# The adaLN partition sums of the dense layer, from float32 vectors or from two float32r limbs

## The chip, the cores and the metric

The kernel runs on one core of one Trainium2 chip. The metric is the device time of one execution in microseconds (us). The engines are TensorE (PE, with PEld for its weight loads), VectorE (DVE), ScalarE (ACT), GpSimd (POOL) and SyncE (SP), whose queue issues nearly all transfers.

## The reference, cut to what matters

A diffusion backbone of two layers works on 256 latent tokens and 256 context tokens of width 1024. Each layer has an adaLN-modulated RMSNorm, a mixer of two branches, a second adaLN-modulated norm and a feed-forward: a dense SwiGLU of width 2816 in layer 0, eight experts in layer 1. The change touches only how the adaLN modulation is summed:

```python
def adaln(cvec, w_mod, b_mod, n_chunks):
    m = jax.nn.silu(cvec) @ w_mod[:, :n_chunks * D_MODEL] + b_mod[:n_chunks * D_MODEL]
    return jnp.split(m, n_chunks, axis=-1)
```

`w_mod` is 2 x 1024 x 6144. There are two conditioning vectors, that of the latent and that of the context tokens; the context needs fewer chunks in layer 1.

## The kernel before

The products of the layers are made in three float32r matmuls each: weights and activations are cut into a high and a low limb (`wh`, `wl` and `hh`, `hl`), and high x high, high x low and low x high are added in PSUM (L212 to L214). A limb pair costs a ScalarE copy to float32r (`wh` L169) and a VectorE subtraction (`wl` L181). A class `Stream` hands out weight halves of 128 columns; the low limb of half i+2 and the high limb of half i+3 are issued behind the matmuls of half i, which are called a group below: 24 matmuls of 512 columns in the gate and up products and in the first two parts of the down product, 18 in the third.

The dense layer runs in three parts of 8, 8 and 6 blocks of 128 hidden columns. In each part, for two blocks at a time, two gate groups end in `sg` (ScalarE, L1189) and two up groups in `af` (VectorE, L1194), `ah` (ScalarE, L1195) and `al` (VectorE, L1196). Then come the down products of the part, which end in additions to `xT` (L1084). Three PSUM banks turn in these products.

Beside this runs the adaLN of later stages, as a background queue (`bgq["mod"]`). Its generator `adaln_units` goes through units of 512 columns of `w_mod`: eight loads of 128 x 512 (`rawm`, L303, 256 KB each, eight buffers), each multiplied by a scalar per partition and accumulated into `acc` on VectorE, once per vector (L318 the first time, then L320). A finished `acc` still has to be summed over the 128 partitions. That is what `finish` does: a matmul (L268) whose stationary operand is a slice of `one_col`, zero but for one column of ones, so that vector m of a list lands in row m of `psr`. When the list is complete, ScalarE copies the rows (`rw`, L273), TensorE transposes them (L278) and VectorE adds the bias into `mod` (L283).

In the dense layer there are three lists (L1165): units (0,10) and (0,11) with two vectors each, (1,0) to (1,3) with two, (1,4) to (1,11) with one; 20 vectors. `finish` for a unit is reached one step after the second load of the next unit, and for the last unit of a list two steps after its last accumulation.

The order of all engines' instructions is written out by the program (a manual schedule). After every three product matmuls `tick` adds `pace["mod"]` to a credit, and at each full unit of credit the generator runs to its next `yield`: one step. At 0.5 that is one step in two ticks. `need(0, 11)` behind the first part's gate and up products and `drain("mod")` behind the down products run what is left at once. The lists take 169 steps, and the layer has 494 ticks ahead of the drain.

Of the kernel before, what the change touches and what calls it, by code (L numbers as in the profile page):

```python
# [11 lines left out]
F32 = mybir.dt.float32  # L12
F32R = mybir.dt.float32r
I32 = mybir.dt.int32
AF = mybir.ActivationFunctionType
OP = mybir.AluOpType
# [54 lines left out]
def ap_of(t, off, pat):  # L71
    return bass.AP(tensor=t.tensor, offset=t.offset + off, ap=pat)
# [3 lines left out]
def hybrid_kernel(ctx, tc, x, c, ctx_in, c_ctx, w_mod, b_mod, norm1_g, norm2_g, w_in, sink, w_fourier,  # L76
# [3 lines left out]
    V, A, P_, G, S = nc.vector, nc.scalar, nc.tensor, nc.gpsimd, nc.sync  # L80
# [6 lines left out]
    const = ctx.enter_context(tc.tile_pool(name="const", bufs=1))  # L87
# [9 lines left out]
    pace = {"attn": 1.0, "mod": 0.5}  # L97
# [130 lines left out]
    one_col = const.tile([128, 15], F32, name="one_col")  # L228
    G.memset(one_col, 0.0)
    G.memset(one_col[:, 7:8], 1.0)  # L230
    mhalf = const.tile([128, 4], F32, name="mhalf")
    G.memset(mhalf, -0.5)

# [3 lines left out]
    mod = [const.tile([128, 48, 2], F32, name=f"mod{l}") for l in range(2)]  # L237
# [12 lines left out]
    g2col = lambda l: cols[:, 112 + l * 8:112 + (l + 1) * 8]  # L250


    def adaln_units(ps_pool, todo, raw_at, nraw, acc_at, nacc, queue, rows=None, may=None):


        total, first, nv0 = sum(t[2] for t in todo), todo[0], todo[0][2]
        gathered = [0, None]

        def finish(l, u, nv, acc):
            if rows:  # L260
                while may and not may():
                    yield
                if gathered[1] is None:
                    gathered[1] = ps_pool.tile([8, 512], F32, name="psr", tag="s", bufs=2)
                ps = gathered[1]
                for v in range(nv):
                    m = gathered[0]
                    P_.matmul(ps[:total, :], one_col[:, 7 - m:7 - m + total], acc[v], start=(m == 0),  # L268
                              stop=(m == total - 1))
                    gathered[0] += 1  # L270
                if gathered[0] == total:
                    rw = rows()
                    A.activation(rw[:total, :], ps[:total, :], AF.Copy)  # L273
                    yield
                    nu = len(todo)
                    pt = ps_pool.tile([128, 4, nu, nv], F32, name="psm", tag="t", bufs=NT_)
                    for ct in range(4):
                        P_.transpose(pt[:, ct].rearrange("p u v -> p (u v)"),  # L278
                                     rw[:total, ct * 128:(ct + 1) * 128], ident[:total, :total])
                    u0 = first[1]  # L280
                    for v in range(nv):
                        as_uc = lambda t: t.rearrange("p (u c) -> p u c", c=4)
                        V.tensor_tensor(as_uc(mod[l][:, 4 * u0:4 * (u0 + nu), v]),  # L283
                                        pt[:, :, :, v].rearrange("p c u -> p u c"),
                                        as_uc(bcol(l)[:, 4 * u0:4 * (u0 + nu)]), op=OP.add)
                    for t in todo:
                        done[t[0], t[1]] = True
                return
            ps = ps_pool.tile([128, 4, 2], F32, name="psm", tag="t", bufs=NT_)
            for ct in range(4):  # L290
                for v in range(nv):
                    P_.matmul(ps[:, ct, v:v + 1], acc[v][:, ct * 128:(ct + 1) * 128], ones[:, 0:1],
                              start=True, stop=True)
            V.tensor_tensor(mod[l][:, 4 * u:4 * u + 4, :nv], ps[:, :, :nv],
                            bcol(l)[:, 4 * u:4 * u + 4, None].to_broadcast([128, 4, nv]), op=OP.add)
            done[l, u] = True
            return
            yield

        def load(i):  # L300
            l, u, nv = todo[i // 8]
            r = raw_at(i)
            queue.dma_start(r, ap_of(w_mod, l * D * NMOD * D + (i % 8) * NMOD * D + u * 512,  # L303
                                 [[KC * NMOD * D, 128], [1, 512]]))
            return r

        late = []
        raws = [load(i) for i in range(nraw)]
        yield
        for i in range(8 * len(todo)):  # L310
            (l, u, nv), kc = todo[i // 8], i % 8
            if kc == 0:
                acc = acc_at(i // 8)
            r = raws.pop(0)
            for v in range(nv):
                s = cvec[:, kc, v:v + 1]
                if kc == 0:
                    V.tensor_scalar(acc[v], r, s, None, op0=OP.mult)  # L318
                else:
                    V.scalar_tensor_tensor(acc[v], r, s, acc[v], op0=OP.mult, op1=OP.add)  # L320
                yield
            if i + nraw < 8 * len(todo):
                raws.append(load(i + nraw))
            if kc == 7:
                if nacc == 1:
                    yield
                    yield from finish(l, u, nv, acc)
                    yield
                    yield
                else:  # L330
                    late.append((l, u, nv, acc))
            if late and kc == 1:
                yield from finish(*late.pop(0))
        yield
        while late:
            yield from finish(*late.pop(0))
# [341 lines left out]
    with ExitStack() as st:  # L678
        ld = st.enter_context(tc.tile_pool(name="ld", bufs=1))
        rows = ld.tile([128, 128], F32, name="rows")  # L680
# [448 lines left out]
    with ExitStack() as st:  # L1129
# [3 lines left out]

        mx_ = [modp.tile([128, 512], F32, name=f"mx{i}") for i in range(4)]
        bgq["mod"].append(adaln_units(psA, [(0, u, 2) for u in (4, 5)], lambda i: mx_[2 + i % 2], 2,
                                      lambda i: mx_[:2], 1, G))

        def more_mod():
            ring = r16.tile([128, 8, T2], F32, name="ring", tag="ro")
            bgq["mod"].append(adaln_units(psA, [(0, u, 2) for u in range(6, 10)], lambda i: ring[:, i % 8, :], 8,  # L1140
                                          lambda i: (mx_[:2], mx_[2:])[i % 2], 2, S,
                                          lambda: rw_of[0].tile([8, 512], F32, name="rw", tag="rw"),
                                          lambda: rw_of))
# [17 lines left out]
        load_tab()  # L1161
        dump("x1", xT)
        modp2 = st.enter_context(tc.tile_pool(name="modp2", bufs=1, side="right"))
        pace["mod"] = 0.5
        for todo in ([(0, u, 2) for u in range(10, 12)], [(1, u, 2) for u in range(4)],  # L1165
                     [(1, u, 1) for u in range(4, 12)]):
            bgq["mod"].append(adaln_units(
                psA, todo, lambda i: modp2.tile([128, 512], F32, name="rawm", tag="rawm", bufs=8), 8,
                lambda i: [modp2.tile([128, 512], F32, name="acc", tag="acc", bufs=4) for _ in range(2)], 2, S,
                lambda: modp2.tile([8, 512], F32, name="rw", tag="rw")))  # L1170
        ff = st.enter_context(tc.tile_pool(name="ff", bufs=1))
        ssum = ff.tile([128, 512], F32, name="ssum", tag="ssum")
        sq = lambda n: ff.tile([128, n], F32, name="sq", tag="sq", bufs=2)
        for a, b in PARTS:
            ah = r16.tile([128, 8, T2], F32R, name="ah", tag="ro")
            al = r16.tile([128, 8, T2], F32R, name="al", tag="ro")
            for j in range(a, b, 2):
                sg = []
                for br in range(2):
                    for k in range(2):  # L1180
                        if j == 0 and br == 0:
                            ps = first[k]
                        else:
                            wh, wl = stream.take()
                            ps = psA.tile([128, 512], F32, name="psp", tag="mm", bufs=3)
# [5 lines left out]
                        else:  # L1191
                            i = j - a + k
# [120 lines left out]
    class Flow:  # L1313
# [24 lines left out]
        def high(self):  # L1338

            if not self.todo:  # L1340
                i = self.n_high
                if i == len(self.us):
                    return
                self.hi[i] = hlp.tile([128, 2048], F32R, name="eh", tag="wh", bufs=3)
                src = self.raw[i].parts(4 if i == len(self.us) - 1 else 2 if i < 2 else 1)
                wd = 2048 // len(src)
                self.todo = [(i, x, slice(wd * k, wd * k + wd), k == len(src) - 1) for k, x in enumerate(src)]
            i, x, sl, last = self.todo.pop(0)
            with self.if_split(i):
                A.activation(self.like(self.hi[i][:, sl], x), x, AF.Copy)  # L1350
            self.owed.append((i, x, sl, last))
            if last:
                self.n_high += 1
# [664 lines left out]
```

## Time and profile before

| | |
|---|---|
| median of 3 runs | 1889.34 us (1888.78 to 1890.16) |
| the profiled execution | 1892.03 us, span 1890.1 us |
| mean granted TensorE clock | 0.987 |
| busy: PE, DVE, ACT, POOL | 1808.0, 1505.8, 1131.6, 64.7 us |
| dense layer | from 369 to 735 us of the span |
| its background sums (first to last) | 401.7 to 623.7 us |

Times in the trace are microseconds from the span's start. In a timeline row the first number is the start and the second the duration (of a run of equal instructions, of all of them); matmuls overlap, so their cost is read from the distances of starts, and not from durations. What stands in brackets is the engine's idle time before the instruction and what ended it.

### The profile page before, as it was taken

Reading aid. Unit: us, or ns where it says so; the run is one execution under the profiler, and the core shown is the slowest. Engines: PE = TensorE matmul, PEld = TensorE weight load, DVE = VectorE, ACT = ScalarE, POOL = GpSimd, SP = SyncE. Lnnn points to the kernel's source line nnn. Section 1 sums busy time; section 2 is a strip of 40 time slices with the busy share of each in tenths; the row PEclk is TensorE's granted clock in tenths of the full one; section 3 lists DMA queues with packets and bytes.
Section 4 is the critical chain, followed back from the end, with each engine's and each line's share of the span. In section 5 each row is a group of like instructions: output and inputs, shape, how many; then the busy total and the mean of one; then the engine's idle time right before and its main releaser. Section 6 shows DMA issues by size and latency. Waiting matters only on the chain. (4 is left out here: it accounts for less than half of the span.)

```text
span 1890.1 us, 27281 instructions
## 1 busy us (share of the span) xinstructions
PE 1808.0 (96%) x9701; PEld 1503.6 (80%) x9701; DVE 1505.8 (80%) x1772; ACT 1131.6 (60%) x1280; POOL 64.7 (3%) x95
## 2 busy tenths in 40 slices
PE   7999999999999999999998999999999999999996
PEld 5788877877777888899877778778887788888874
DVE  6788896578777335787788998999889988889897
ACT  5664522422122223665487878888778887787785
POOL 3200000200000001100000000000000000000000
PEclk9999999999999999999899999999999999999998
DMA  9323463265577223434889999999999999999993
GB/s 297 104 58 98 134 202 100 95 213 187 178 241 249 90 79 100 135 112 141 305 331 343 387 364 375 408 403 408 353 344 406 399 399 336 337 356 376 368 403 125
DMA packets 223312, 488.57 MB, mean 258 GB/s; under 512 B 11426, under 2 KB 107938, under 8 KB 223140
## 3 DMA queue, kind: packets, MB, share of 16 engines
q1 hardware_dynamic: 221860, 482.11, 70.5%
q0 software_dynamic: 1280, 4.20, 0.8%
q8 instruction: 105, 1.72, 0.4%
q14 instruction: 67, 0.55, 0.1%
HBM read 485.22 MB, written 1.05 MB: 257 GB/s over the span
## 5 line engine op out<-in xcount | busy, mean ns | idle before, releaser
L1374 DVE TENSOR_TENSOR el<-raw,eh 128x2048 fp32r<-128x2048 f32 (+2 forms) x332 | 723.8, 2210 | 85.7 <-ACT eh L1350 76.9
L1350 ACT ACTIVATE eh<-raw 128x2048 fp32r<-128x2048 f32 (+2 forms) x332 | 607.6, 1858 | 95.2 <-PE pgt L1831 63.8
L212 PE MATMUL psp<-hh,wh 128*128 128x512 f32 (+1 forms) x704 | 260.8, 370 | 2.6 <-ACT U L954 1.8
L214 PE MATMUL psp<-hh,wl 128*128 128x512 f32 (+1 forms) x704 | 256.1, 364 | 4.9 <-DVE wl L181 4.8
L213 PE MATMUL psp<-hl,wh 128*128 128x512 f32 (+1 forms) x704 | 255.3, 363 | 0.0
L181 DVE TENSOR_TENSOR wl<-raw,wh 128x1024 fp32r<-128x1024 f32 (+1 forms) x152 | 182.3, 1206 | 41.8 <-PE psp L214 20.8
L169 ACT ACTIVATE wh<-raw 128x1024 fp32r<-128x1024 f32 (+1 forms) x152 | 156.4, 1039 | 61.2 <-DMA raw<-in_w_down_d 24.7
L212 PEld LDWEIGHTS psp<-hh,wh 128*128 128x128 f32 x704 | 134.3, 191 | 30.9 <-issue 9.9
L214 PEld LDWEIGHTS psp<-hh,wl 128*128 128x128 f32 x704 | 134.1, 190 | 27.9 <-DVE wl L181 7.4
L213 PEld LDWEIGHTS psp<-hl,wh 128*128 128x128 f32 x704 | 134.2, 191 | 19.2 <-issue 0.5
L1831 PE MATMUL py<-el,eah 128*128 128x256 f32 (+1 forms) x712 | 125.7, 314 | 8.3 <-DVE el L1374 7.3
L1831 PEld LDWEIGHTS py<-el,eah 128*128 128x128 f32 x712 | 101.7, 189 | 36.4 <-DVE el L1374 28.1
L1831 PE MATMUL py<-eh,eah 128*128 128x512 f32 x440 | 120.6, 396 | 0.0
L320 DVE SCALAR_TENSOR_TENSOR acc<-rawm,cvec,acc 128x512 f32<-128x512 f32 x140 | 99.8, 747 | 1.4
L1831 PE MATMUL pup<-el,xh 128*128 128x256 f32 (+1 forms) x560 | 94.4, 307 | 4.6 <-DVE el L1374 4.5
L1831 PEld LDWEIGHTS pup<-el,xh 128*128 128x128 f32 x560 | 80.7, 188 | 19.6 <-DVE el L1374 11.1
L1831 PE MATMUL pgt<-el,xh 128*128 128x256 f32 (+1 forms) x480 | 84.9, 315 | 11.3 <-DVE el L1374 10.7
L1831 PE MATMUL pup<-eh,xh 128*128 128x512 f32 x336 | 94.0, 401 | 0.0
L1831 PEld LDWEIGHTS pgt<-el,xh 128*128 128x128 f32 x480 | 70.1, 191 | 27.6 <-DVE el L1374 19.6
L1831 PEld LDWEIGHTS py<-eh,eah 128*128 128x128 f32 x440 | 78.7, 188 | 14.4 <-ACT eh L1350 0.8
L1831 PE MATMUL pgt<-eh,xh 128*128 128x512 f32 x296 | 83.4, 404 | 0.7 <-ACT xh L1462 0.7
L1195 ACT ACTIVATE ah<-af 128x512 fp32r<-128x512 f32 x22 | 13.9, 632 | 99.8 <-DVE af L1194 99.8
(379 smaller groups left out, 3236.1 us busy)
## 6 DMA issues: line engine op xcount, KB each, us to landing
raw<-in_w_gate_e SPq DMA_DIRECT2D x111, 1024.0 KB, 7.5
raw<-in_w_down_e SPq DMA_DIRECT2D x110, 1024.0 KB, 8.0
raw<-in_w_up_e SPq DMA_DIRECT2D x109, 1024.0 KB, 8.3
rawm<-in_w_mod SPq DMA_DIRECT2D x112, 256.0 KB, 5.3
raw<-in_w_in SPq DMA_DIRECT2D x26, 1024.0 KB, 5.4
raw<-in_w_gate_d SPq DMA_DIRECT2D x11, 1024.0 KB, 5.3
raw<-in_w_up_d SPq DMA_DIRECT2D x11, 1024.0 KB, 5.5
mraw<-in_w_mod SPq DMA_DIRECT2D x16, 512.0 KB, 8.4
```

The costliest lines, as they stand in the source:

```text
L169: A.activation(h[:, :n, :], src, AF.Copy)
L181: self.eng.tensor_tensor(lo[:, :n, :], src, h[:, :n, :].bitcast(F32), op=OP.subtract)
L212: P_.matmul(ps, wh[:, k, :], ah, start=(start and i == 0), stop=False)
L213: P_.matmul(ps, wh[:, k, :], al, start=False, stop=False)
L214: P_.matmul(ps, wl[:, k, :], ah, start=False, stop=(stop and i == n - 1))
L320: V.scalar_tensor_tensor(acc[v], r, s, acc[v], op0=OP.mult, op1=OP.add)
L1195: A.activation(ah[:, i, :], t, AF.Copy)
L1350: A.activation(self.like(self.hi[i][:, sl], x), x, AF.Copy)
L1374: V.tensor_tensor(self.like(self.lo[i][:, sl], x), x, self.like(self.hi[i][:, sl], x).bitcast(F32), op=OP.subtract)
L1831: P_.matmul(ps[:, a:b], x[:, k, :], w[:, c + a:c + b], start=(start and ps_id[i] not in seen), stop=(stop and ps_id[i] not in ps_id[i + 1: ...
```

## The change

The vectors of the dense layer are cut into two float32r limbs before they are summed: a ScalarE copy makes the high one, a VectorE subtraction the low one, out of a ring of three buffers `limb`. Two steps later two float32r matmuls per vector, with a float32r copy of `one_col` as the stationary operand, take the place of the float32 one. The pace of the background queue in the dense layer goes from 0.5 to 0.55. The sums of the mixer, which use the same function, stay as they are.

```diff
@@ -228,6 +228,8 @@
     one_col = const.tile([128, 15], F32, name="one_col")
     G.memset(one_col, 0.0)
     G.memset(one_col[:, 7:8], 1.0)
+    one_row = const.tile([128, 15], F32R, name="one_row")
+    V.tensor_copy(one_row, one_col)
@@ -250,7 +252,7 @@
-    def adaln_units(ps_pool, todo, raw_at, nraw, acc_at, nacc, queue, rows=None, may=None):
+    def adaln_units(ps_pool, todo, raw_at, nraw, acc_at, nacc, queue, rows=None, may=None, high=None):
@@ -265,8 +267,17 @@
                 for v in range(nv):
                     m = gathered[0]
-                    P_.matmul(ps[:total, :], one_col[:, 7 - m:7 - m + total], acc[v], start=(m == 0),
-                              stop=(m == total - 1))
+                    x = [(one_col, acc[v])]
+                    if high:
+                        hi, lo = high()
+                        A.activation(hi, acc[v], AF.Copy)
+                        V.tensor_tensor(lo, acc[v], hi.bitcast(F32), op=OP.subtract)
+                        x = [(one_row, hi), (one_row, lo)]
+                        yield
+                        yield
+                    for i, (one, a) in enumerate(x):
+                        P_.matmul(ps[:total, :], one[:, 7 - m:7 - m + total], a, start=(m == 0 and i == 0),
+                                  stop=(m == total - 1 and i == len(x) - 1))
                     gathered[0] += 1
@@ -1161,13 +1172,14 @@
-        pace["mod"] = 0.5
+        pace["mod"] = 0.55
...
-                lambda: modp2.tile([8, 512], F32, name="rw", tag="rw")))
+                lambda: modp2.tile([8, 512], F32, name="rw", tag="rw"),
+                high=lambda: [modp2.tile([128, 512], F32R, name="limb", tag="limb", bufs=3) for _ in range(2)]))
```

## Rows read from the trace of the kernel before

**Rows 1.** The page's first part: busy us, share of the span, instructions.
```profile
PE 1808.0 (96%) x9701; PEld 1503.6 (80%) x9701; DVE 1505.8 (80%) x1772; ACT 1131.6 (60%) x1280; POOL 64.7 (3%) x95
```

**Rows 2.** By stretch: length, busy PE, PEld, DVE, ACT, POOL; clock, DMA share, GB/s.
```profile
401.40:452.60 51.20, 51.20 (x219) 39.21 (x218) 37.28 (x53) 14.91 (x19) 0.00 (x0) 1.00 0.54 180
...
500.30:597.50 97.20, 97.20 (x405) 72.45 (x404) 69.17 (x95) 24.27 (x31) 0.00 (x0) 1.00 0.70 233
...
1100.00:1400.00 300.00, 286.35 (x1593) 240.56 (x1592) 270.56 (x172) 240.58 (x200) 0.00 (x0) 1.00 0.99 379
```

**Rows 3.** Waits from 379 to 640: who for whom, us in total, times, longest.
```profile
DVE al L1196 <- ACT ah L1195: 11.2, 16, 0.7
...
PEld psp L214 <- DVE wl L181: 2.1, 3, 1.2
...
PE psp L214 <- DVE wl L181: 0.8, 1, 0.8
```

**Rows 4.** Instructions of tile psr, 379 to 640: ns min/median/max, first and last start.
```profile
L268 PE MATMUL psr<-acc,one_col x40: 592/592/597, 401.7 to 623.7; 128*8 128x512 f32 x32, 128*4 128x512 f32 x8
L273 ACT ACTIVATE rw<-psr x3: 588/588/588, 423.3 to 624.4; 8x512 f32<-8x512 f32 x2, 4x512 f32<-4x512 f32 x1
```

**Rows 5.** Timeline of PE around the first pair and up to the second.
```profile
401.39 0.39 PE L214 MATMUL psp<-hh,wl 128*128 128x512 f32 x1
401.71 1.88 PE L268 MATMUL psr<-acc,one_col 128*4 128x512 f32 x4
...
403.86 0.40 PE L213 MATMUL psp<-hl,wh 128*128 128x512 f32 x1
...
421.11 0.39 PE L214 MATMUL psp<-hh,wl 128*128 128x512 f32 x1
```

**Rows 6.** Timeline of PE around a single vector.
```profile
539.92 0.39 PE L214 MATMUL psp<-hh,wl 128*128 128x512 f32 x1
...
541.53 0.39 PE L213 MATMUL psp<-hl,wh 128*128 128x512 f32 x1
```

**Rows 7.** Timeline of PE in the start-up: float32r matmuls with four stationary columns.
```profile
46.39 0.39 PE L811 MATMUL psq<-hl,wh 128*128 128x512 f32 x1
46.61 0.28 PE L716 MATMUL psg<-mh,c 128*4 128x256 f32 x1
...
47.90 0.28 PE L716 MATMUL psg<-ml,c 128*4 128x256 f32 x1
```

**Rows 8.** Groups by line, 379 to 640: busy us, mean ns, idle before.
```profile
L320 DVE SCALAR_TENSOR_TENSOR acc<-rawm,cvec,acc 128x512 f32<-128x512 f32 x140 | 99.8, 747 | 1.4
...
L1196 DVE TENSOR_TENSOR al<-af,ah 128x512 fp32r<-128x512 f32 x16 | 11.1, 693 | 11.2 <-ACT ah L1195 11.2
...
L1195 ACT ACTIVATE ah<-af 128x512 fp32r<-128x512 f32 x16 | 10.1, 632 | 74.1 <-DVE af L1194 74.1
```

**Rows 9.** Timeline of DVE at the start of the layer's accumulations.
```profile
379.49 0.88 DVE L318 TENSOR_SCALAR acc<-rawm,cvec 128x512 f32<-128x512 f32 x2 [8.15 <-DMA rawm<-in_w_mod]
...
392.51 1.21 DVE L181 TENSOR_TENSOR wl<-raw,wh 128x1024 fp32r<-128x1024 f32 x1
393.64 2.73 DVE L320 SCALAR_TENSOR_TENSOR acc<-rawm,cvec,acc 128x512 f32<-128x512 f32 x4
```

**Rows 10.** Timeline of PE at the same place.
```profile
382.23 0.50 PE L214 MATMUL psp<-hh,wl 128*128 128x512 f32 x1 [0.79 <-DVE wl L181]
```

**Rows 11.** Timeline of DVE, 406 to 426 us.
```profile
406.57 0.69 DVE L1194 TENSOR_TENSOR af<-sg,psp 128x512 f32<-128x512 f32 x1
407.96 0.69 DVE L1196 TENSOR_TENSOR al<-af,ah 128x512 fp32r<-128x512 f32 x1 [0.70 <-ACT ah L1195]
...
425.26 0.24 DVE L283 TENSOR_TENSOR mod<-psm,cols 128x8 f32<-128x8 f32 x2 [8.38 <-PE psm L278]
```

**Rows 12.** Timeline of DVE from the span's start: its first instruction.
```profile
5.01 0.18 DVE L700 TENSOR_TENSOR c<-cvec,c 128x16 fp32r<-128x16 f32 x1 [5.01 <-ACT c L699]
```

**Rows 13.** Waits of SP's queue, 735 to 905: the first expert loads (L1224).
```profile
SPq L1224 <- PE psp L214: 4.9, 4, 3.7
```

## The prediction

> **What bounds the kernel now.** I read the page's busy times first [rows 1], then the busy times by stretch [rows 2], then who waited for whom between 379 and 640 us [rows 3], and last the order of time around single places. The reader is to see this. TensorE is busy for 96% of the span [rows 1], but that is an average; what counts is the dense layer, where the change sits. There TensorE is busy for all of 51.20 us and all of 97.20 us at the full granted clock (1.00, the 2.4 GHz level), while VectorE is busy 71 to 73% and ScalarE 25 to 29% [rows 2]. In 261 us TensorE and its weight loads wait for VectorE's low limbs for 2.1 + 0.8 us only [rows 3]. So in this stage a TensorE microsecond removed is a microsecond of the kernel, as long as the other two engines stay ahead.
>
> **Removed: the float32 sums.** Between 401.7 and 623.7 us the profile has 40 instructions `psr<-acc,one_col` of float32 [rows 4]: 20 vectors, two instructions each. Their price is what they push apart. The ordinary rate first: from the L213 at 403.86 to the L214 at 421.11 lie 76 product matmuls, (421.11 - 403.86)/76 = 0.227 us each [rows 5]. A pair of vectors: from the L214 at 401.39 to the L213 at 403.86 are 2.47 us, in which two ordinary matmul steps lie (0.454), so the pair costs 2.016 us [rows 5]. A single vector: 539.92 to 541.53 is 1.61, less 0.454, 1.156 us [rows 6]. The units (0,10), (0,11) and (1,0) to (1,3) are pairs, (1,4) to (1,11) are single: 6 x 2.016 + 8 x 1.156 = 21.3 us. A pair has two instructions more than a single vector and costs 2.016 - 1.156 = 0.860 more, 0.430 each; 40 of them are 17.2 us. What is left of a single one, 1.156 - 0.860 = 0.296, comes once for each of 14 insertions, 4.1 us in all: the switch between float32r and float32.
>
> **Added on TensorE: 40 float32r matmuls**, 128 x 512 with a stationary of 4 or 8 columns. The trace has float32r matmuls with 4 columns and 256 moving columns: from 46.61 to 47.90 us eleven steps, 0.117 us each, and the step from a product matmul to the first of them is 0.22 us, an ordinary one [rows 7]. So few columns cost no extra and there is no switch. For 512 columns I take the 0.227 of the products: 40 x 0.227 = 9.1 us. Net on TensorE: 21.3 - 9.1 = 12.2 us less. The dear end of this price is that each insertion keeps its 0.296 us, and there are now 20 insertions, since every vector of a pair stands alone: 9.1 + 5.9 = 15.0, net 6.3. I take the first, by the nearest row.
>
> The rows show a float32 vector of 512 columns as two instructions of 0.430 us [rows 5, 6]. The Trainium skill (FP8 and Floating Point Precision, section TensorE Precision Notes) says that true FP32 takes four passes through the array; 2 x 0.430 against 0.227 for one pass agrees. By passes alone, four made into two, the gain would be 40 x (0.430 - 0.227) = 8.1 us and the switches would stay; the rows give more, because they show a switch that has no reason left.
>
> **Added on ScalarE and VectorE:** 20 copies to float32r and 20 subtractions. The same shapes are in the layer: `ah` 632 ns and `al` 693 ns [rows 8], so 12.6 and 13.9 us. Both lie beside TensorE, in 25 to 29% and 71 to 73% of busy time. What isn't free is order. The subtraction waits for the copy, as `al` waits 0.70 us for `ah` sixteen times [rows 3]. Behind it on VectorE stand the accumulations, `wl`, `af`; TensorE waits for `wl`, and SyncE's weight loads wait for it too. Here the copy can run early: a vector is complete some two to four accumulations before its limbs are issued (four run in 2.73 us, one lasts 747 ns: (2.73 - 0.75)/3 = 0.66 apart [rows 8, 9]), and ScalarE mostly idles.
>
> The cover for TensorE is the two added yields. A mod step comes each 1/0.55 = 1.8 ticks and a tick is three matmuls, 0.68 us, so 9 to 12 matmuls, 2.0 to 2.7 us, lie between the issue of the limbs and their matmuls. VectorE needs 0.7 us after it gets there, so it may be some 1.3 to 2.0 us behind TensorE's place. Is it? It often leads (before the transposes of `psm` it waits 8.38 us [rows 11]); it is latest just after an `af` group: there `af` starts at 406.57, when TensorE's group ends, and `al` ends at 407.96 + 0.69 = 408.65, some 2 us into the next group [rows 11]. Counting steps by the code (the same count gives 78 matmuls between the first two psr of before, and the trace has 78), the matmuls fall 132, 144, 225, 237, 366, 378, 477, 486, 585, 597, 678, 690, 765, 819, 873, 930, 984, 1038, 1092 and 1140 product matmuls into the layer. Only at 144, 237 and 819 does the limb stand near behind such a chain, and there 3 to 9 matmuls more than the chain lie between. I put one 0.70 us wait there; the ends are 0 and 3 x 1.4 = 4.2 (copy and subtraction bare at each).
>
> The three limb buffers make a second wait: the low limb of a pair's second vector reuses the first's high limb, so VectorE stands until TensorE has used it, and its lead of a few us is gone six times. That costs TensorE nothing while the next need is 12 matmuls away; a `wl` is needed a whole group (24 matmuls, 5.4 us) after its place.
>
> **Moved: pace 0.55 and later sums.** VectorE starts the layer's accumulations late, at 379.49, for a DMA, and lags; TensorE waits for `wl` (the L214 at 382.23 [rows 10]), and VectorE stays late until the `wl` of 392.51 [rows 9]. By the count of steps the first two groups hold four steps as before, the third one more: 0.66 us. The units need 40 more steps, 380 ticks in place of 338; the last transposes come at matmul 1146 instead of 1020. The check for unit (0,11) falls at 336 and it is ready at 240, and the drain at 1482, so no lump runs at the end. The copy of the psr rows (588 ns [rows 4]) has now 3 matmuls' cover at two of three places where it had 6: it ends 1.0 us after the last sum begins, and TensorE is there at 0.9 to 1.0. 0.2 us each, 0.4. The one-time copy of `one_row` stands ahead of VectorE's first instruction, which waits until 5.01 us for ScalarE [rows 12]: nothing. SyncE's 256 KB loads are the same in number and spread wider; no price.
>
> **Sum:** -21.3 + 9.1 + 0.7 + 0.7 + 0.4 = -10.4 us. The profiled execution lasted 1892.0 us (span 1890.1 and 1.9 around it), so it would become 1881.6; the median of the runs is 2.7 below that execution, so 1889.3 - 10.4 = **1878.9 us**. What comes behind moves with it: the first expert loads wait for product matmuls of the mixer ahead of them, not for a time of their own [rows 13].
>
> **Rivals.** (a) *The limbs come late* at the `af` groups: up to 4.2 us in place of 0.7, 1882.4. For it: `al` waits every time. Against: VectorE's leads. (b) *The switch stays* with each insertion: net 6.3 - 1.8, 1884.8; [rows 7] speak against it. (c) *Passes alone count*, the case of four passes to two: 8.1 - 1.8, 1883.0. (d) *Given back among the experts*, where DMA is busy 0.99 of the time [rows 2]: 1889.3. It would need loads that are not released by the work before them. (e) *VectorE becomes the bound*, slower. Per group of 24 matmuls (5.45 us) it does a `wl` (1.21 [rows 9]), half of `af`, wait and `al` (2.08/2 = 1.04), and of 4.4 steps 3.5 accumulations (2.3) and 0.44 subtractions: 4.55 + 0.44 x (0.69 + w), where w is the wait of one low limb. With w = 0.7 that is 5.2; above 1.35 it is more than TensorE's 5.45. With w = 2.7, the whole 12 matmuls of a buffer's turn at every vector, it is 6.04, and 48 groups x 0.59 = 28 us are lost: 1889.3 - 12.2 + 28 = 1905. Against it: only the second vectors of six pairs wait for TensorE, and copies run early. (f) *It does not do what it says*: float32r with few columns running as two instructions each, 80 x 0.43 = 34.4 against 17.2, 1889 + 13 to 17, some 1904; [rows 7] speak against it.
>
> **Chances.** Forecast 0.66, (a) 0.10, (b) 0.06, (c) 0.04, (d) 0.06, (e) 0.05, (f) 0.03. A measurement of this kernel tells about 0.2%, 3.8 us, from no change. Faster by more: forecast, a, b, c, 0.86; same: d, 0.06; slower: e and f, 0.08. Range: the low end is the whole 12.2 us and the 0.6 by which the fastest run lies under the median, 1876.5; the high end takes in (a), (b) and (c), and half a microsecond of spread, 1885.3. (d), (e), (f) are left out, 0.14.
>
> **What would show it.** After: psr as 40 float32r instructions 0.227 apart, no step of 0.5 behind them; TensorE busy without a gap from 401 to 640; hardly any wait of psr for a limb; the layer's last transposes about 18 us later than 625 in its own time (126 matmuls more, less the gain) and the first expert load some 10 us earlier. I am wrong if psr waits for `limb` in total several us, if `wl` waits of TensorE grow past the first groups, or if the first expert load is 10 us earlier and the end is not.

## The result and the profile after

The changed kernel takes 1878.46 us (median of 5, 1877.18 to 1879.81) against 1889.34 (1888.53 to 1891.67): a ratio of 0.994, 95% interval 0.9927 to 0.9954, or 10.9 us less. The forecast was 1878.9, with a range from 1876.5 to 1885.3.

The first reading is the list of waits between 379 and 660 us (who for whom, us in total, times, longest), the answer to [rows 3]:

```profile
ACT limb L273 <- DVE acc L331: 24.5, 8, 6.0
...
DVE limb L274 <- PE psr L279: 9.6, 3, 4.1
...
DVE limb L274 <- ACT limb L273: 4.3, 4, 2.8
PEld psp L214 <- DVE wl L181: 2.7, 3, 1.2
PE psp L214 <- DVE wl L181: 1.4, 2, 0.7
```

No line of that list has TensorE's `psr` waiting for a limb. ScalarE's 24.5 us are waits for vectors that were not yet complete: its queue had come to the copy first. VectorE waits for TensorE (three times, for the buffer of an earlier limb) and for ScalarE; all of this is beside the path. TensorE's own waits are for `wl`, as before.

What took the place of the float32 sums, by the timeline of TensorE around the first vector (start, duration), which answers [rows 5] and [rows 6]:

```profile
401.61 0.39 PE L213 MATMUL psp<-hl,wh 128*128 128x512 f32 x1
401.83 0.39 PE L214 MATMUL psp<-hh,wl 128*128 128x512 f32 x1
402.06 0.63 PE L279 MATMUL psr<-limb,one_row 128*4 128x512 f32 x2
402.53 0.39 PE L212 MATMUL psp<-hh,wh 128*128 128x512 f32 x1
402.76 0.40 PE L213 MATMUL psp<-hl,wh 128*128 128x512 f32 x1
```

From the L214 at 401.83 to the L213 at 402.76 are 0.93 us. Two ordinary steps of 0.227 taken off, a vector costs 0.476 us, where before a single one cost 1.156. The sum begins 0.23 us after the product ahead of it, one ordinary step: the switch is gone. Read in the same way at every place, the sums of the layer cost 21.3 us before and 9.4 after, 11.9 less.

The instructions of tile `psr` and its limbs (ns min/median/max, first and last start):

```profile
L279 PE MATMUL psr<-limb,one_row x40: 391/397/398, 402.1 to 642.0; 128*8 128x512 f32 x32, 128*4 128x512 f32 x8
L273 ACT ACTIVATE limb<-acc x20: 613/625/635, 396.9 to 636.9; 128x512 fp32r<-128x512 f32 x20
L274 DVE TENSOR_TENSOR limb<-acc,limb x20: 679/684/693, 400.7 to 637.6; 128x512 fp32r<-128x512 f32 x20
```

The busy times by stretch (columns as in [rows 2]); the first two lines are of before, the dense layer up to the next norm's first `psb`, then the mixer of layer 1 up to the first expert load:

```profile
369.40:743.40 374.00, 372.11 (x1630) 291.25 (x1629) 233.50 (x334) 96.87 (x123) 0.69 (x1) 1.00 0.52 171
743.40:895.90 152.50, 145.54 (x1063) 139.18 (x1064) 115.95 (x248) 92.05 (x186) 14.67 (x21) 0.96 0.40 125
```

and the same two of after:

```profile
369.90:732.70 362.80, 360.30 (x1631) 293.49 (x1630) 245.25 (x354) 108.29 (x143) 0.69 (x1) 1.00 0.54 176
732.70:880.70 148.00, 140.09 (x1063) 133.33 (x1064) 115.70 (x248) 92.07 (x186) 14.62 (x21) 1.00 0.41 129
```

The dense layer is 11.2 us shorter: the 11.9 at the sums, less 0.7 that the faster pace costs in the first groups (below). VectorE's busy time in it rises by 11.8 and ScalarE's by 11.4 us, and costs nothing beyond that 0.7. The mixer, whose instructions are the same, is 4.5 us shorter too, at a granted clock of 1.00 instead of 0.96. That is why the two profiled spans differ by 14.6 us (1890.1 and 1875.5) and the medians by 10.9 only: the profile of before was one of the longer runs, that of after one of the shorter. The experiments below show that the mixer's part isn't the change's.

The experts move as they are. The first expert load is issued at 895.93 us before and at 880.72 after (timelines of SyncE's queue, before and then after):

```profile
895.93 2.59 SPq L1224 DMA_DIRECT2D raw<-in_w_gate_e  x4
```

```profile
880.72 3.55 SPq L1236 DMA_DIRECT2D raw<-in_w_gate_e  x4
```

From there to the span's end are 994.2 us before and 994.8 after.

### The profile page after: what moved, and what is told of

Its sections match the earlier page's. It is cut to its first block, busy times and chain, and to the rows that moved or that the text cites. A ratio compares the mean times of both kernels' runs of the same rounds, so it can differ in the third digit from the quotient of the medians.

```text
span 1875.5 us, 27319 instructions
## 1 busy us (share of the span) xinstructions
PE 1790.7 (95%) x9701; PEld 1497.7 (80%) x9701; DVE 1517.4 (81%) x1793; ACT 1143.0 (61%) x1300; POOL 64.3 (3%) x95
## 5 line engine op out<-in xcount | busy, mean ns | idle before, releaser
L214 PE MATMUL psp<-hh,wl 128*128 128x512 f32 (+1 forms) x704 | 255.1, 362 | 5.4 <-DVE wl L181 5.4
L213 PE MATMUL psp<-hl,wh 128*128 128x512 f32 (+1 forms) x704 | 254.4, 361 | 0.0
L214 PEld LDWEIGHTS psp<-hh,wl 128*128 128x128 f32 x704 | 132.9, 189 | 28.3 <-DVE wl L181 8.0
L213 PEld LDWEIGHTS psp<-hl,wh 128*128 128x128 f32 x704 | 133.2, 189 | 19.6 <-issue 0.5
L1843 PE MATMUL pgt<-el,xh 128*128 128x256 f32 (+1 forms) x480 | 84.5, 314 | 11.2 <-DVE el L1386 10.7
L1843 PEld LDWEIGHTS py<-eh,eah 128*128 128x128 f32 x440 | 78.6, 188 | 14.6 <-ACT eh L1362 0.8
```

Of the source, the lines that this page charges most:

```text
L213: P_.matmul(ps, wh[:, k, :], al, start=False, stop=False)
L214: P_.matmul(ps, wl[:, k, :], ah, start=False, stop=(stop and i == n - 1))
L1843: P_.matmul(ps[:, a:b], x[:, k, :], w[:, c + a:c + b], start=(start and ps_id[i] not in seen), stop=(stop and ps_id[i] not in ps_id[i + 1: ...
```

## The experiments

The theory was that TensorE's own order of work sets the end of the dense layer, with a price for each instruction: 0.227 us for a float32r matmul, 0.430 for a float32 instruction, 0.296 for a switch; the two yields keep the limbs ahead of it. The rivals: that passes alone count, that the pace did it, that VectorE limits, and that the gain comes from elsewhere.

A length of the dense layer below is taken from the trace of the kernel: from the start of the last matmul of the layer's first products (before: 369.36 us) to the start of the next norm's first `psb` in the last ones (before: 743.40). It tells tenths of a microsecond, where medians tell some 2. Ratios are to the kernel before on the same chip (medians 1890.8 for the two paces, each vector alone and the high limb alone, 1890.18 for the other four).

| kernel | dense layer, us | mixer, us | median, us | ratio, 95% interval |
|---|---|---|---|---|
| before | 374.05 | 152.5 | 1889.34 | |
| after | 362.82 | 148.1 | 1878.46 | 0.9940 (0.9927 to 0.9954) |
| pace 0.5 with limbs | 362.17 | 152.4 | 1878.64 | 0.9935 (0.9918 to 0.9953) |
| pace 0.55, float32 | 374.90 | 148.6 | 1890.86 | 1.0007 (0.9996 to 1.0018) |
| each vector alone, float32 | 376.42 | 149.4 | 1891.61 | 1.0003 (0.9992 to 1.0015) |
| high limb alone | 357.99 | 150.2 | 1873.84 | 0.9913 (0.9897 to 0.9930) |
| low limb three times | 371.88 | 148.7 | 1885.35 | 0.9970 (0.9959 to 0.9981) |
| no yields | 373.27 | 148.1 | 1886.65 | 0.9980 (0.9970 to 0.9990) |
| six limb buffers | 362.91 | 150.4 | 1877.20 | 0.9924 (0.9904 to 0.9944) |
| layer 0's mixer too | 363.05 | 149.6 | 1884.05 | 0.9963 (0.9948 to 0.9977) |

### What the pace does

```diff
-        pace["mod"] = 0.55
+        pace["mod"] = 0.5
```

> The limbs as in the changed kernel, but the pace of the background queue left at 0.5. Theory (TensorE's own order sets the dense layer's end; 0.227 us a float32r matmul, 0.430 a float32 instruction, 0.296 a switch): the extra accumulation that made TensorE wait 0.66 us more for a low weight limb in the layer's first groups is gone, the 209 steps end after 418 of 494 ticks, nothing else moves: 1877.8 us, 0.0 to 1.0 under the changed kernel. Rival (VectorE is near its limit and the faster pace costs throughout): 3 us or more under the changed kernel. Rival (the faster pace is needed, the queue runs out of ticks): slower than the changed kernel by a lump of several us before the drain.

The median is that of the changed kernel (0.2 us over it, which no run here can tell from nothing). The dense layer is 0.65 us shorter. The timeline of TensorE in the changed kernel shows where the faster pace costs it:

```profile
388.04 0.39 PE L213 MATMUL psp<-hl,wh 128*128 128x512 f32 x1
389.13 0.50 PE L214 MATMUL psp<-hh,wl 128*128 128x512 f32 x1 [0.70 <-DVE wl L181]
```

The step is 1.09 us. VectorE has five accumulations ahead of the `wl` in question:

```profile
384.54 3.40 DVE L331 SCALAR_TENSOR_TENSOR acc<-rawm,cvec,acc 128x512 f32<-128x512 f32 x5
```

The kernel before has four there, in 2.73 us. With pace 0.5 the same step of TensorE is 0.43 us, as in the kernel before:

```profile
387.20 0.39 PE L213 MATMUL psp<-hl,wh 128*128 128x512 f32 x1
387.63 0.50 PE L214 MATMUL psp<-hh,wl 128*128 128x512 f32 x1
```

The mixer took 152.4 us here, as before, with the same clock of 0.96, though the limbs are in:

```profile
369.00:731.20 362.20, 360.32 (x1631) 293.54 (x1630) 245.52 (x354) 107.55 (x143) 0.69 (x1) 1.00 0.53 177
731.20:883.60 152.40, 145.48 (x1063) 139.13 (x1064) 116.16 (x248) 91.97 (x186) 14.46 (x21) 0.96 0.39 125
```

So the mixer's 4.5 us follow the granted clock of the run, not the change.

The reverse, the pace alone in the kernel before:

> The kernel before with the pace 0.55 alone, float32 sums as they were. Theory: TensorE's work is the same, the first groups wait 0.66 us more: 1890.0 us, the same as before within the measurement. Rival (part of the gain of the change came from the pace, by spreading the sums otherwise): 1885 or less.

The same as before within the measurement; the dense layer is 0.85 us longer. The pace brings nothing by itself. Here the mixer ran at a clock of 0.99 and took 148.6 us, with float32 sums: the same conclusion from the other side.

### What a float32 insertion costs

```diff
-                        hi, lo = high()
-                        A.activation(hi, acc[v], AF.Copy)
-                        V.tensor_tensor(lo, acc[v], hi.bitcast(F32), op=OP.subtract)
-                        x = [(one_row, hi), (one_row, lo)]
                         yield
                         yield
```

> Two yields ahead of each vector's sum and pace 0.55 as in the changed kernel, but no limbs: one float32 matmul per vector, each vector alone. It has 40 float32 instructions as before, but 20 insertions instead of 14. Theory (a switch between float32r and float32 costs 0.296 us per insertion): 6 x 0.296 = 1.8 us of TensorE more than before in the dense layer, and 0.7 for the pace: 1891.8 us; in the trace each vector pushes the product matmuls 1.156 us apart. Rival (passes alone count, the rest belongs to a first sum of a list): 1890.0.

The median says 1891.61, where 1891.8 was expected, but its interval holds the kernel before; the trace decides. Against the kernel with the pace alone the dense layer is 376.42 - 374.90 = 1.5 us longer, for six more insertions of the same 40 instructions, 0.25 each where 0.296 was the price. Added up at the sums alone, the distances are 23.1 us against 21.3: 1.8 for the six, the price itself; the 0.3 that the length lacks lies in steps between products elsewhere in the layer. Passes alone would have given 0. In the timeline of TensorE each vector pushes its neighbours apart as the single ones of before did:

```profile
400.71 0.39 PE L214 MATMUL psp<-hh,wl 128*128 128x512 f32 x1
401.03 1.02 PE L275 MATMUL psr<-acc,one_col 128*4 128x512 f32 x2
401.98 0.50 PE L212 MATMUL psp<-hh,wh 128*128 128x512 f32 x1
402.32 0.39 PE L213 MATMUL psp<-hl,wh 128*128 128x512 f32 x1
```

400.71 to 402.32 is 1.61, less 0.454: 1.156 us. That is what the float32r pair of the changed kernel does in 0.476.

### What a float32r matmul costs

```diff
-                        x = [(one_row, hi), (one_row, lo)]
+                        x = [(one_row, hi)]
```

> As the changed kernel, but the low limb, though made, is not summed: 20 float32r matmuls instead of 40 (a part of the sum is left out). Theory (each float32r matmul costs 0.227 us and TensorE sets the end): 20 x 0.227 = 4.5 us less than the changed kernel, 1873.9. Rival (what was gained is limited by VectorE's or ScalarE's added work): no difference to the changed kernel.

1873.84 us, 4.6 under the changed kernel; the dense layer is 4.8 us shorter, 0.24 for each of 20 matmuls. ScalarE's and VectorE's work was all there, so it isn't they that limit.

```diff
-                        x = [(one_row, hi), (one_row, lo)]
+                        x = [(one_row, hi), (one_row, lo), (one_row, lo), (one_row, lo)]
```

> As the changed kernel, but the low limb is summed three times, four float32r matmuls per vector (the sum is not the reference's). Theory: 40 matmuls more at 0.227 to 0.233 us, 9.1 to 9.3 us over the changed kernel, 1887.7. Rival (TensorE has slack in the layer that swallows short work): less than 3 us over it.

The dense layer is 371.88 - 362.82 = 9.06 us longer, 0.227 for each of 40 matmuls. The median rose by 6.9 (1885.35), less than the 9.1 of the trace; it is 8.2 over the kernel with six buffers (below), which ran on the same chip. Its runs range from 1883.4 to 1891.1, and the mixer took up to 4.5 us more where its clock was lower. Both edits say that a matmul put in or taken out here is paid in full.

### What the two yields cover

```diff
                         x = [(one_row, hi), (one_row, lo)]
-                        yield
-                        yield
```

> As the changed kernel, without the two yields: the float32r matmuls of a vector stand right behind the issue of its limbs. Theory (the yields are the cover of the chain copy, subtraction, matmul; VectorE's and ScalarE's lead over TensorE hides most of it anyway): TensorE waits for the second vectors of the six pairs, whose low limb needs the buffer that the matmul just before gives back (0.7 us of subtraction less 0.2 of the other matmul, 6 x 0.5 = 3 us), and 0.7 to 1.4 us at a few more places behind an up group: 3 to 8 us over the changed kernel, 1882 to 1886, with waits of psr for limb in the profile. Rival (the cover is not needed): as the changed kernel, 1878.5. Rival (VectorE is always behind): 20 x 1.4 = 28 us over it.

1886.65 us, a little beyond the end of what the theory gave; the dense layer is 10.5 us longer than in the changed kernel and nearly as long as before. All but 0.8 us of the layer's gain is lost. Of the 10.5 us, 9.7 stand at the sums themselves. (Without the yields the queue also has 40 steps less, so the sums fall at other places than in the changed kernel.) The waits between 379 and 640 us:

```profile
PEld psr L277 <- DVE limb L274: 11.9, 17, 1.5
...
PE psr L277 <- DVE limb L274: 4.5, 12, 1.0
...
PEld psr L277 <- ACT limb L273: 3.7, 3, 1.7
...
PE psr L277 <- ACT limb L273: 2.4, 3, 1.3
```

(PE and PEld wait for the same thing, so their figures are not added.) One place in time, of TensorE:

```profile
509.31 0.39 PE L214 MATMUL psp<-hh,wl 128*128 128x512 f32 x1
510.22 0.40 PE L277 MATMUL psr<-limb,one_row 128*8 128x512 f32 x1 [0.53 <-ACT limb L273]
510.94 0.63 PE L277 MATMUL psr<-limb,one_row 128*8 128x512 f32 x2 [0.33 <-DVE limb L274]
511.77 0.40 PE L277 MATMUL psr<-limb,one_row 128*8 128x512 f32 x1 [0.20 <-DVE limb L274]
```

I had counted on ScalarE's and VectorE's lead and priced the second vectors of pairs and a few places. The first sum found its high limb late here. The weight load of a low sum waited for its limb at 17 of 20 vectors, and its matmul stood idle for it at 12: the copy and the subtraction come one after the other, and TensorE's high sum covers only 0.23 us of the subtraction's 0.68.

### Does the ring of three buffers matter

```diff
-tag="limb", bufs=3)
+tag="limb", bufs=6)
```

> As the changed kernel, with six limb buffers instead of three, so that no limb waits for a matmul just issued. Theory: VectorE's 9.6 us of waiting for psr go, but they lie beside TensorE, which gains nothing: as the changed kernel within 0.5 us. Rival (the ring of three costs TensorE time through VectorE's lost lead): 2 us or more under it.

VectorE's 9.6 us of waiting for `psr` are gone from the list of waits, and the dense layer is 362.91 us, 0.1 longer. The median, 1877.20 of four runs, lies within the spread. The wait was free, as the theory has it.

### The same edit in layer 0's mixer

```diff
-        pace.update(attn=1.0, mod=0.65)
+        pace.update(attn=1.0, mod=0.75)
...
-                                          lambda: rw_of))
+                                          lambda: rw_of,
+                                          high=lambda: [rw_of[0].tile([128, 512], F32R, name="limb", tag="limb",
+                                                                      bufs=3) for _ in range(2)]))
```

> As the changed kernel, and the eight vectors that layer 0's mixer sums in float32 (four pairs between 245 and 301 us) are made from limbs too, with the queue's pace there raised from 0.65 to 0.75. TensorE is relieved of 4 x 2.016 - 16 x 0.23 = 4.4 us. Theory: TensorE is busy without a gap there as well, but VectorE is busy 14.3 of 15 and 19.7 of 20 us in that stretch, so eight subtractions of 0.69 us with their waits and the faster pace find no room: between no gain and 4 us slower than the changed kernel, 1878 to 1882. Rival (VectorE's busy share does not matter as long as TensorE has its weights two groups ahead): the whole 4.4 us, 1874.1.

1884.05 us: 5.6 over the changed kernel, worse than the theory's own bound. The dense layer kept its gain (363.05), but it begins at 374.47 us instead of 369.85. The waits between 240 and 320 us:

```profile
ACT xh L1084 <- DVE th L1083: 21.0, 7, 4.4
...
PEld psr L279 <- ACT limb L273: 5.5, 4, 1.6
...
PE psr L279 <- ACT limb L273: 3.8, 4, 1.2
...
PEld psr L279 <- DVE limb L274: 2.6, 4, 0.6
PE psm L289 <- ACT rw L284: 2.3, 1, 2.3
```

and three of the places on TensorE:

```profile
309.48 0.39 PE L279 MATMUL psr<-limb,one_row 128*8 128x512 f32 x1 [1.19 <-ACT limb L273]
310.21 0.40 PE L279 MATMUL psr<-limb,one_row 128*8 128x512 f32 x1 [0.33 <-DVE limb L274]
314.28 0.41 PE L289 MATMUL psm<-ident,rw 8*128 8x8 f32 x4 [2.32 <-ACT rw L284]
```

TensorE waits first for the copy. ScalarE is busy about a third of that stretch, yet late: its queue stands behind `xh`, which waits 21.0 us in all for VectorE's `th`. Its timeline ahead of the sum at 309.48:

```profile
308.28 0.63 ACT L1084 ACTIVATE xh<-th 128x512 fp32r<-128x512 f32 x1 [1.61 <-DVE th L1083]
308.82 0.61 ACT L273 ACTIVATE limb<-mx 128x512 fp32r<-128x512 f32 x1
```

A late VectorE thus makes ScalarE late too, and the cover of two yields is too short. By its share VectorE was not full: it is busy for 68.1 of these 80 us, and for 64.6 in the changed kernel (there 19.2 of 20 from 260 to 280, 11.6 of 20 from 300 to 320). The waits for limbs fall at 266 to 272 and at 305 to 311 us, so the share that the expectation went by doesn't tell where limbs come late. How much of the loss is the limbs' and how much the faster pace's is not shown: they were not tried apart.

## Why the prediction was right, point by point

*The bound.* TensorE sets the end of the dense layer: a matmul added there was paid with 0.227 us and one taken out with 0.24, and 11.4 us of ScalarE's and 11.8 us of VectorE's busy time, put in beside it, cost nothing; the first groups' 0.7 is the pace's. The 2.1 + 0.8 us of waiting that the prediction read from [rows 3] count the same waits twice, once for the weight load and once for the matmul; either figure is small.

*The removed sums.* The 21.3 us were the prices 0.430 and 0.296. The kernel with each vector alone shows the same 1.156 per vector, and its six insertions more cost 1.8 us at the sums, as priced (1.5 in the layer's length). Of the gain some 4 us are the switches, which a count of passes leaves out.

*The added matmuls.* 0.476 us was measured at the first vector where 0.454 was taken; all twenty together are 9.4 us instead of 9.1. The start-up's float32r matmuls with four columns [rows 7] were the right row.

*The first groups.* 0.66 us were forecast and 0.65 is the difference to pace 0.5. The place was wrong: the extra step falls in the second group (the wait at 389.13), not in the third. My count began with an empty credit; with 0.40 to 0.44 in it, as the mixer may have left (the credit is not reset), the same count gives all twenty places of the trace, the first after 129 matmuls instead of 132. At 0.5 every credit below 0.5 gives the same places, so the row of before couldn't show it.

*The waits.* One wait of 0.7 us for a limb and two of 0.2 for the copied rows were put into the sum. None came: TensorE never waits for `limb`, and the first transposes start one ordinary switch (0.32) behind the matmul ahead of them. These 1.1 us too much and the 0.4 too little at the matmuls make the sum -10.4 where the dense layer's trace says -11.2. That the forecast lies within 0.4 us of the median is thus in part luck: these errors offset each other in part, the medians moved by 0.3 us less than the layer, and the runs of the changed kernel spread over 2.6.

*The rest.* Nothing was given back: the first expert load came earlier by more than the forecast's 10 us, since the mixer's clock added to it, and from there to the end the span was the same within 0.6 us. The last transposes came at 643.7 us, 18 later than before, as forecast.

*The rivals.* Late limbs: they are real without the yields (10.5 us) and in layer 0's mixer, and absent in the change. The switch that stays, and passes alone: excluded by the rows above. VectorE as the bound: 9.6 us of waiting for the ring of buffers cost nothing, as six buffers show. Float32r without effect: excluded.

## What to carry to other kernels

Where TensorE is busy without a gap, price an edit by how far apart the neighbouring instructions start, with the step into and out of a different type counted, since those steps were about a third of what was saved (4.1 of 11.2 us). Limbs made on two other engines are free only as long as their chain is issued well ahead: here 9 to 12 matmuls of cover were worth 10 us, and the same edit, with a faster pace, lost time in layer 0's mixer. There a chain through a lightly busy engine was late, since that engine's queue stood behind something that waited for VectorE.

## What the runs showed of the hardware that I had not expected

Layer 1's mixer, the same instructions in nearly all of these kernels, took 148.1 to 152.5 us. Its length went with the granted clock: 152.5 and 152.4 us at a mean of 0.96 (before, pace 0.5), 150.4 at 0.98 (six buffers), 148.6 at 0.99 (pace 0.55), 148.1 at 1.00 (after). In before the largest fall is in this stretch,

```profile
750.00:765.00 15.00, 14.76 (x89) 14.20 (x90) 10.40 (x30) 9.38 (x16) 10.89 (x16) 0.77 0.14 50
```

behind 15 us in which TensorE was busy for 12.6, with two steps of 1.15 us between matmuls in the norm. After has the same steps there, and about the same place stayed at the full 2.4 GHz level:

```profile
739.00:754.00 15.00, 13.62 (x99) 12.63 (x100) 12.68 (x31) 10.79 (x19) 12.07 (x16) 1.00 0.16 54
```

So the same gaps are followed by a lower clock in one run and not in another. What decides it these runs do not show. By this stretch alone, the profiles of kernels with the same mixer differ by up to 4.5 us, nearly half of what the change saves.
